# Recurrence scores by head parity: two 64-row products in two PSUM banks for one 128-row product over zeroed halves

## The chip, the cores and the metric

One core of one Trainium2 chip runs the whole program in one launch. The time is device microseconds from start to end. Three runs of the kernel before took 2598.1, 2588.69 and 2594.0 us, median 2594.0.

Engine names are those of the profile: PE is TensorE's matrix products, PEld its weight loads, DVE VectorE, ACT ScalarE, POOL GpSimd, SP SyncE. SP computes nothing here; it issues nearly all DMA transfers, in the order of its queue. The waits and counts of instructions are read from the profile and from the order in which the program lists each engine's instructions.

## The reference

One step of a two-layer decoder trunk: sliding-window attention, then RWKV-7 time mixing, over one prompt of 2048 tokens (16 learned meta tokens ahead of it) and a sample batch of 8 sequences of 4 tokens with a given state. The change lies in the time mixing. For every head (16 heads of 64) it runs a recurrence over the tokens:

```
def step(S, inp):
    r_t, w_t, k_t, v_t, a_t, b_t = inp
    sa = jnp.einsum('bhvk,bhk->bhv', S, a_t)
    S = S * w_t[:, :, None, :] + sa[..., None] * b_t[:, :, None, :] + v_t[..., None] * k_t[:, :, None, :]
    return S, jnp.einsum('bhvk,bhk->bhv', S, r_t)
```

Here w, k, v, r, a and b come from projections of the normalised input. After it come a group norm, a bonus term, a SiLU gate, the output projection, the residual add and the final norm.

## The kernel before

The program has three stages: the attention layer, the projections of the time mixing (their results go to DRAM), and from about 1600 us on the recurrence with everything behind it.

**Units and chunks.** The recurrence runs in chunks of 32 tokens, since inside a chunk it can be written as matrix products. There are 17 prompt units in order: unit 0 (kind `m`, 32 rows with the meta tokens) and units 1 to 16 (kind `p`, 128 tokens, four chunks each), and one sample unit (kind `s`). A unit goes through these steps:

1. `load_vectors` (L892 to L914) loads, for all heads, BK (the b and k vectors, 64 columns a chunk, two heads on 128 partitions: the head's parity e says which half) and L, one tile for a block of two chunks. L holds the a and r vectors of a head on the 64 partitions of its parity; the other 64 partitions are set to zero on POOL (L911, at raised priority, two memsets of 64x1024 for each block, four a unit).
2. `scores` (L930 to L955) multiplies BK with L for each pair of heads: K is 128 (both heads), and the zeroed halves keep the heads apart, so that the 128 columns of the result are the 64 scores of each head. Half of a block (four pairs) fills one PSUM bank `pz`. ACT copies one quadrant of it to LAs (32x128, eight copies a block), and DVE writes the masked scores to the half of L that was zero (64x256, eight operations a block). From here on L is one operand of 128 rows for the chain.
3. `inverse` (L957 to L1009): SP stores LAs to DRAM (`la_d<-LAs`, two transfers) and loads it back with one 32x32 matrix of a head and chunk on each partition (`LA<-la_d`, two). POOL multiplies by norms (`LA<-LA,ln`), makes the inverse of the unit triangular matrices in 31 steps of two operations each (`XT<-LA,X`, then `X<-X,XT`), and multiplies by norms again (`X<-X,ln`). SP stores the result (`tt_d<-X`, two transfers). Units 1 and 2 are done on DVE.
4. `elementwise` (L1302) drives steps 1 to 3 for a unit ahead and loads the inverse back as `TT<-tt_d`, two transfers of 64x512.
5. `keys` (L1342 to L1360) transposes BK on PE (L1357) into a bank `kt` of a PSUM pool `pk` of its own, and ACT copies it to LS.
6. `chain` (L1388) does a chunk: C = L times the state Z on PE, R0s by ACT, the solve `C<-R0s,TT` with the unit's inverse, the result into Z by ACT, then the new state `C<-Z,LS` on PE and its decay on DVE. `outputs` multiplies L with Z into Y.

**What sets the order.** The main loop (L1690 and below) goes through units and chunks. Beside unit i it puts in the group norm and gate of unit i - 1, the output projection of unit i - 2 (chunks 0 and 1; its end has three small `ms` operations on POOL, L1639, at raised priority) and, as `ahead`, the scores and inverse of unit i + 2. POOL therefore works on the inverse of one unit while PE runs the chain of an earlier one. The final order of each engine's instructions, SP's queue included, is decided by a scheduler when the program is built, from priorities, dependencies and free buffers; each engine then runs its list in order. An issue on SP that has to wait holds back everything behind it in SP's list. SP's issues also use eight semaphores in turn, so an issue waits until the one eight places ahead of it has landed.

**PSUM.** In the recurrence: `pz` one bank (scores), `pk` one (key copies), `pf` two (projections), `pr` four (C0, C1, Y0, Y1). Scores of the first units borrow banks of `pf` and `pr` (`bank`, L1259).

Of the kernel before, what the change touches and what calls it, by code (L numbers as in the profile page):

```python
# [30 lines left out]
def tile_hybrid_step(ctx: ExitStack, tc: tile.TileContext, a, o, c):  # L31
# [5 lines left out]
    def mm(out, lhsT, rhs, start, stop, **kw):  # L37
        return t_.matmul(out=out, lhsT=lhsT, rhs=rhs, start=start, stop=stop, **kw).ins  # L38
# [4 lines left out]
    def tt(e, out, in0, in1, op):  # L43
        return e.tensor_tensor(out=out, in0=in0, in1=in1, op=op).ins  # L44
# [844 lines left out]
    def load_vectors(u):  # L889

        u.BK, u.L = [], []
        if u.kind != "p":  # L892
            room = wl.tile([P, 2, 2 * KC * 64], F32, name="rooml", tag="L", bufs=nbuf["L"])
            u.spare = room[:, 1, 512:768].rearrange("p (g v) -> p g v", v=64)
            u.BKs = room[:, 1, 0:512].rearrange("p (h g c x) -> p h g c x", h=2, g=4, c=1)
        for half in range(2):
            hs = slice(half * 4, half * 4 + 4)
            BK = es.tile([P, 4, 4, 64], F32, name="BK", tag="BK", bufs=nbuf["BK"]) if u.kind == "p" else u.BKs[:, half]
            dma(BK, bk_d[u.blk][:, hs, u.c0:u.c0 + u.nch, :])
            u.BK.append(BK)  # L900
        for c2 in range(u.np):
            if u.kind == "p":
                L = wl.tile([P, 2, 2, KC, 64], F32, name="L", tag="L", bufs=nbuf["L"])
            else:
                L = room[:, 0].rearrange("p (e c g x) -> p e c g x", e=2, c=1, g=KC)
            u.L.append(L)
            w, c0 = min(2, u.nch - 2 * c2), u.c0 + 2 * c2
            for e, ps_ in HS:

                with tc.high_priority(offset=5000):  # L910
                    g_.memset(L[OS[e], e], 0.0)  # L911
                dma(L[ps_, e].rearrange("p c g x -> p (c g x)"), ar_d[u.blk][ps_, c0:c0 + w].rearrange("p c g x -> p (c g x)"))
            yield 0.8

# [15 lines left out]
    def scores(u, c2):  # L930

        nch = u.nch
        mk = smk_s if u.kind == "s" else smk
        w = min(2, nch - 2 * c2)
        L = u.L[c2]
        for half in range(2):
            hs = slice(half * 4, half * 4 + 4)
            BK = u.BK[half]
            ps = bank(u)
            for j in range(4):  # L940
                for cc in range(w):
                    u.scored = mm(ps[64 * cc:64 * cc + 64, j], BK[:, j, 2 * c2 + cc, :], L[:, :, cc, half * 4 + j, :], True, True)
            for cc in range(w):
                r0 = 64 * cc
                for e in range(2):
                    la = u.LAs[32 * (1 - e):32 * (1 - e) + 32, half, 2 * c2 + cc]
                    if u.kind == "s":
                        tt(v_, la, ps[r0:r0 + 32, :, e, 0:32], smk_a[r0:r0 + 32, None, :].broadcast_to([32, 4, 32]), ALU.mult)
                    else:
                        act(la, ps[r0:r0 + 32, :, e, 0:32])  # L950
            for cc in range(w):
                r0 = 64 * cc
                for e in range(2):
                    tt(v_, L[OS[e], e, cc, hs, :], ps[r0:r0 + 64, :, e, :],
                       mk[r0:r0 + 64, None, :].broadcast_to([64, 4, 64]), ALU.mult)  # L955

    def inverse(u, room=None, ln=None):  # L957

# [61 lines left out]
    with ExitStack() as ph:  # L1020
# [144 lines left out]
        for x, b in enumerate(order):  # L1165
# [39 lines left out]
            if follow is None:  # L1205

                if delay:
                    todo.append((b, prv))
                    rest_v = rest_values()
                    fill(rest_v, V0)  # L1210
                wrx.close()
                es = wrx.enter_context(tc.tile_pool(name="es", bufs=1, side="right", reuse_waits="tile"))
                wl = wrx.enter_context(tc.tile_pool(name="wl", bufs=1, side="right", reuse_waits="tile"))
                for u in us[:PRE]:
                    for _ in load_vectors(u):
                        pass
                if nblk > 2:
                    bank = lambda u: pd.tile([P, 4, 2, 64], F32, name="pz", tag="pd")
                    las = wk.tile([P, 2048], F32, name="las", tag="dx", bufs=1)
                    room1 = wk.tile([P, 2, 1024], F32, name="room1", tag="xn", bufs=1)  # L1220
                    for i, x0, room in ((1, 0, room1), (0, 1024, None)):
                        u = us[i]
                        u.LAs = las[:64, x0:x0 + 256 * u.nch].rearrange("p (h c g i) -> p h c g i", h=2, g=4, i=32)
                        for c2 in range(u.np):
                            scores(u, c2)
                        inverse(u, room, las[:, x0 + 1024 - 32:x0 + 1024] if i == 0 else las[:, 1536:1568])
# [19 lines left out]
    with ExitStack() as ph:  # L1246
# [1 line left out]
        zs = ph.enter_context(tc.tile_pool(name="zs", bufs=1, reuse_waits="tile"))  # L1248
        wk = ph.enter_context(tc.tile_pool(name="wk3", bufs=1, reuse_waits="tile"))
        cs = ph.enter_context(tc.tile_pool(name="c3", bufs=1, reuse_waits="tile"))  # L1250
        pz = ph.enter_context(tc.tile_pool(name="pz", bufs=1, space=PSUM, reuse_waits="tile"))
        pk = ph.enter_context(tc.tile_pool(name="pk", bufs=1, space=PSUM, reuse_waits="tile"))
        pf = ph.enter_context(tc.tile_pool(name="pf", bufs=2, space=PSUM, reuse_waits="tile"))
        pr = ph.enter_context(tc.tile_pool(name="pr", bufs=1, space=PSUM, reuse_waits="tile"))
        SQ = 1
        early = [0]

        def bank(u):
            if u.idx >= PRE:  # L1259
                return pz.tile([P, 4, 2, 64], F32, name="pz", tag="pz")  # L1260
            early[0] += 1
            place_, tag = ((pf, "pd"), (pr, "Y0"), (pr, "Y1"), (pz, "pz"))[early[0] % 4]
            return place_.tile([P, 4, 2, 64], F32, name="pz", tag=tag)


        w_g, w_o = [], []
# [78 lines left out]
        def keys(u, c2):  # L1345

            w = min(2, u.nch - 2 * c2)
            if u.kind == "s":
                u.LS[c2] = [u.room[:, 1]]
            else:  # L1350
                u.LS[c2] = [LSs[(LScount[0] + cc) % 4] for cc in range(w)]
                LScount[0] += 2
            for half in range(2):
                hs = slice(half * 4, half * 4 + 4)
                ps = pk.tile([P, 4, 2, 64], F32, name="kt", tag="kt", bufs=1)
                for j in range(4):
                    t_.transpose(out=ps[:w * 64, j].rearrange("p e d -> p (e d)"),  # L1357
                                 in_=u.BK[half][:, j, 2 * c2:2 * c2 + w, :].rearrange("p c x -> p (c x)"), identity=ident)
                for cc in range(w):
                    for e in range(2):  # L1360
                        act(u.LS[c2][cc][OS[e], e, hs, :], ps[cc * 64:cc * 64 + 64, :, e, :])
# [147 lines left out]
        def new_state(u, old_state, ums, outs, so, Z, LS):  # L1509
            tags = [0]  # L1510

            def bank():

                places = [(pz, "pz"), (pk, "kt")] + ([(pr, "C0"), (pr, "C1")] if over else [])
                tags[0] += 1
                place_, tag = places[tags[0] % len(places)]
                return place_.tile([P, 4, P], F32, name="ns", tag=tag, bufs=1)

            for gr in range(KC):
                ST = old_state(gr, bank())  # L1520
                um = ums[gr % 2]
                for e in range(2):
                    tt(v_, um[OS[e]], Z[OS[e], e, gr, None, :].broadcast_to([64, NB, 64]),
                       bmk[OS[e]].unsqueeze(2).broadcast_to([64, NB, 64]), ALU.mult)
                Sp = bank().rearrange("p a b -> p (a b)")
                for e, ps_ in HS:
                    mm(Sp[ps_], LS[OS[e], e, gr, :], um[OS[e]].rearrange("p b v -> p (b v)"), True, True)
                tt(v_, ST, ST, Sp.rearrange("p (b v) -> p b v", v=64), ALU.add)
                tt(v_, ST, ST, u.pe[:, gr, :].unsqueeze(2).broadcast_to([P, NB, 64]), ALU.mult)
                ps = bank()  # L1530
                for bp in range(4):
                    t_.transpose(out=ps[:, bp, :], in_=ST[:, 2 * bp:2 * bp + 2].rearrange("p b v -> p (b v)"), identity=ident)
                sl = outs[gr % 2]
                act(sl.rearrange("p b e k -> p (b e k)"), ps.rearrange("p a b -> p (a b)"))
                for b2 in range(2):
                    for e in range(2):
                        g_.dma_start(out=so[b2, :, gr, :, e], in_=sl[b2 * 64:b2 * 64 + 64, :, e])
                if gr % 2 == 1:
                    yield 0.8
# [326 lines left out]
```

## Time and profile before

| | before |
|---|---|
| three runs, us | 2598.1, 2588.69, 2594.0 (median 2594.0) |
| profiled execution, us | 2605.2 |
| its span, us | 2603.1 |
| mean granted TensorE clock | 0.962 |
| PE busy, share of the span | 2345.8 us, 90% |
| DVE | 1666.8 us, 64% |
| ACT | 1218.3 us, 47% |
| POOL | 1121.7 us, 43% |
| POOL from 1812 to 2337 us (ten units) | 386.25 of 525 us |

How to read it: the profile is of one execution, so its own time (2605.2) stands beside the span that its rows cover. "Busy" counts instructions that compute, not waits. A row of a list of waits says which engine and tile waited, for what, for how long in all, how often, and the longest. A chain of waits follows the work back from an end to what released each step; its shares are shares of the stretch that was asked for. A row of the time line has start, duration, engine, line, operation, tiles and count, and in brackets the idle time before it with what ended it. A line such as L44 or L50 is that of a helper (`tt`, `dma`), so tiles tell more than lines. Numbers behind a tile's name are left out in the profile.

### The profile page before, as it was taken

The page shows a single profiled execution, that of the slowest core. Times are in us where ns is not written, and L with a number is a line of the kernel's source. Part 1 is how long each engine was busy: PE and PEld are TensorE (multiplying, and loading weights), DVE is VectorE, ACT ScalarE, POOL GpSimd, SP SyncE. Part 2 cuts the span into 40 slices and gives each one's busy share as a digit, 9 for nine tenths or more (in the row PEclk, how much of TensorE's full clock was granted, in tenths as well). Part 3 has the DMA queues.
Part 4 walks back from the last instruction along what each step waited for, and adds up shares of the span by engine and source line. Part 5 has one row for each costly group of instructions (what it writes and reads, how often), then busy time and mean ns, then how long its engine had stood idle before and what let it go on. Part 6 is the DMA issues. An engine that isn't in the chain of part 4 may idle for free.

```text
span 2603.1 us, 59317 instructions
## 1 busy us (share of the span) xinstructions
PE 2345.8 (90%) x23876; PEld 1630.3 (63%) x23876; DVE 1666.8 (64%) x3264; ACT 1218.3 (47%) x2994; POOL 1121.7 (43%) x1640
## 2 busy tenths in 40 slices
PE   6999999899999897999999998769889998899897
PEld 5877777777844445676667776446555555555553
DVE  6587674667748887666565655755565556555664
ACT  6676455565523334454344434344445443544432
POOL 4242122232112344433333325256777777766603
PEclk9999998999999998999999998889999999999898
DMA  8433222332447564322222227575444554454323
GB/s 201 122 106 111 64 74 70 130 98 73 156 113 235 201 224 141 107 85 86 102 93 86 83 84 191 140 190 131 116 116 125 126 128 106 121 129 124 80 56 83
DMA packets 346230, 312.88 MB, mean 120 GB/s; under 512 B 205546, under 2 KB 282218, under 8 KB 344131
## 3 DMA queue, kind: packets, MB, share of 16 engines
q1 hardware_dynamic: 344339, 305.30, 40.8%
q0 software_dynamic: 1616, 3.79, 0.6%
q8 instruction: 188, 3.08, 0.5%
q14 instruction: 87, 0.71, 0.1%
HBM read 191.15 MB, written 119.84 MB: 119 GB/s over the span
## 4 chain that ended last, share of the span: by engine, by line
PE 31%; POOL 21%; DVE 20%; DMA 11%; ACT 8%; issue 7%; SPq 3%; POOLq 0%; ACTq 0%; DVEq 0%
PE pd L38 22%; POOL X L44 6%; POOL XT L44 6%; DVE xm L47 5%; SPq L50 3%; DMA LA<-la_d 2%; DVE xpr L44 2%; PE po L38 2%; ACT ssb L41 2%; POOL var L44 2%; POOL L L911 2%; PE C L38 1%; DMA wst<-in_rwkv_w_in 1%; DMA x<-in_x_prompt 1%; PE sc L38 1%
## 5 line engine op out<-in xcount | busy, mean ns | idle before, releaser
L38 PEld LDWEIGHTS <-yp 128*128 128x128 f16 x1488 | 140.4, 99 | 168.1 <-issue 12.3
L47 DVE SCALAR_TENSOR_TENSOR xm<-dx,mu,xn 128x256 f32<-128x256 f32 (+2 forms) x432 | 200.3, 523 | 48.3 <-POOL dx L44 47.1
L44 POOL TENSOR_TENSOR XT<-LA,X 128x126 f32<-128x126 f32 (+24 forms) x458 | 199.1, 435 | 33.7
L44 POOL TENSOR_TENSOR X<-X,XT 128x126 f32<-128x126 f32 (+24 forms) x458 | 199.0, 435 | 32.8
L38 PE MATMUL pd<-wg,xg 128*128 128x512 f16 (+1 forms) x816 | 199.8, 391 | 0.0
L38 PE MATMUL pd<-xp,wq 128*128 128x256 f16 (+2 forms) x1728 | 186.3, 266 | 13.9 <-DVE qp L47 8.9
L38 PE MATMUL pd<-xp,wg 128*128 128x256 f16 (+2 forms) x1728 | 188.7, 271 | 1.2 <-DVE xp L44 0.8
L38 PE MATMUL po<-wo,yp 128*128 128x512 f16 x768 | 187.5, 387 | 0.6 <-DVE yp L47 0.6
L38 PE MATMUL pd<-wvv,xpr 128*128 128x512 f16 (+1 forms) x816 | 186.9, 386 | 0.0
L38 PE MATMUL pd<-xpr,w 128*128 128x256 f16 (+2 forms) x1728 | 186.3, 267 | 0.0
L44 POOL TENSOR_TENSOR ssb<-ssb,bias 128x512 f32<-128x512 f32 x64 | 86.3, 1354 | 221.8 <-DVE ssb L462 178.3
L38 PEld LDWEIGHTS <-wq 128*128 128x128 f16 x1728 | 159.4, 99 | 35.6 <-DVE qp L47 10.4
L38 PE MATMUL pd<-xpr,wkk 128*128 128x256 f16 (+2 forms) x1728 | 179.5, 264 | 0.0
L38 PEld LDWEIGHTS <-wg 128*128 128x128 f16 x1728 | 162.2, 101 | 25.2 <-issue 4.5
L38 PEld LDWEIGHTS <-w 128*128 128x128 f16 x1728 | 157.7, 99 | 27.1 <-issue 9.7
L38 PEld LDWEIGHTS <-wkk 128*128 128x128 f16 x1728 | 158.2, 98 | 15.6 <-issue 0.4
L44 POOL TENSOR_TENSOR ps<-wst,ps 128x1024 f16<-128x1024 f32 x32 | 69.4, 2169 | 226.6 <-ACT wst L41 207.5
L38 PE MATMUL pd<-w,yp 128*128 128x512 f16 x720 | 162.3, 383 | 3.8 <-DMA yp<-y 3.8
L44 DVE TENSOR_TENSOR Z<-C,pe 64x256 f32<-64x256 f32 x256 | 107.8, 421 | 68.2 <-PE C L38 62.1
L38 PEld LDWEIGHTS <-xpr 128*128 128x128 f16 (+1 forms) x816 | 78.6, 100 | 101.8 <-issue 16.5
L44 DVE TENSOR_TENSOR L<-pz,smk 64x256 f32<-64x256 f32 x256 | 108.0, 422 | 47.8 <-ACT LAs L41 29.4
L44 DVE TENSOR_TENSOR xpr<-xm,xpr 128x512 f16<-128x512 f32 (+2 forms) x144 | 98.5, 705 | 57.3 <-ACT xpr L41 57.0
(358 smaller groups left out, 4983.4 us busy)
## 6 DMA issues: line engine op xcount, KB each, us to landing
wst<-in_rwkv_w_in SPq DMA_DIRECT2D x32, 512.0 KB
wsp<-ps SPq DMA_DIRECT2D x32, 512.0 KB
BK<-bk SPq DMA_DIRECT2D x32, 512.0 KB
L<-ar SPq DMA_DIRECT2D x64, 256.0 KB
x<-in_x_prompt SPq DMA_DIRECT2D x29, 512.0 KB
xn<-xn SPq DMA_DIRECT2D x14, 1028.0 KB
ar<-aro SPq DMA_DIRECT2D x28, 512.0 KB
bk<-bko SPq DMA_DIRECT2D x28, 512.0 KB
```

The costliest lines, as they stand in the source:

```text
L38: return t_.matmul(out=out, lhsT=lhsT, rhs=rhs, start=start, stop=stop, **kw).ins
L41: return s_.activation(out=out, in_=in_, func=func, **kw).ins
L44: return e.tensor_tensor(out=out, in0=in0, in1=in1, op=op).ins
L47: v_.scalar_tensor_tensor(out=out, in0=in0, scalar=scalar, in1=in1, op0=op0, op1=op1)
L50: return nc.sync.dma_start(out=out, in_=in_).ins
L911: g_.memset(L[OS[e], e], 0.0)
```

## The change

The zeroed halves are no longer written: L911 and its priority block go. `scores` multiplies only the 64 partitions of one head at a time (K is 64, 64 columns), twice as many products, the two parities in turn, each into its own bank, so that a block needs two banks at once where half a block needed one. ACT and DVE then work on whole blocks: four copies of 32x256 and four masked writes of 64x512 a block instead of eight of each. The PSUM pool `pz` gets two banks and takes over the key copies of `pk`, which goes. `bank` becomes `banks`; the sample's state update uses the two banks of `pz` where it used `pz` and `pk`.

```diff
             for e, ps_ in HS:
-                with tc.high_priority(offset=5000):
-                    g_.memset(L[OS[e], e], 0.0)
                 dma(L[ps_, e].rearrange("p c g x -> p (c g x)"), ar_d[u.blk][ps_, c0:c0 + w].rearrange("p c g x -> p (c g x)"))
...
-        for half in range(2):
-            hs = slice(half * 4, half * 4 + 4)
-            BK = u.BK[half]
-            ps = bank(u)
-            for j in range(4):
-                for cc in range(w):
-                    u.scored = mm(ps[64 * cc:64 * cc + 64, j], BK[:, j, 2 * c2 + cc, :], L[:, :, cc, half * 4 + j, :], True, True)
+        pss = banks(u)
+        for g in range(KC):
             for cc in range(w):
...
-                    la = u.LAs[32 * (1 - e):32 * (1 - e) + 32, half, 2 * c2 + cc]
...
-                        act(la, ps[r0:r0 + 32, :, e, 0:32])
...
+                for e, ps_ in HS:
+                    u.scored = mm(pss[e][64 * cc:64 * cc + 64, g, :], u.BK[g // 4][ps_, g % 4, 2 * c2 + cc, :], L[ps_, e, cc, g, :], True, True)
+        for cc in range(w):
+            r0 = 64 * cc
+            for e in range(2):
+                la = u.LAs[32 * (1 - e):32 * (1 - e) + 32, :, 2 * c2 + cc]
+                sc = pss[e][r0:r0 + 32, :, 0:32].rearrange("p (h g) i -> p h g i", h=2)
...
+                    act(la, sc)
+        for cc in range(w):
+            r0 = 64 * cc
+            for e in range(2):
+                tt(v_, L[OS[e], e, cc], pss[e][r0:r0 + 64], mk[r0:r0 + 64, None, :].broadcast_to([64, KC, 64]), ALU.mult)
...
-        pz = ph.enter_context(tc.tile_pool(name="pz", bufs=1, space=PSUM, reuse_waits="tile"))
-        pk = ph.enter_context(tc.tile_pool(name="pk", bufs=1, space=PSUM, reuse_waits="tile"))
+        pz = ph.enter_context(tc.tile_pool(name="pz", bufs=2, space=PSUM, reuse_waits="tile"))
...
-        def bank(u):
-            if u.idx >= PRE:
-                return pz.tile([P, 4, 2, 64], F32, name="pz", tag="pz")
+        def banks(u):
             early[0] += 1
-            place_, tag = ((pf, "pd"), (pr, "Y0"), (pr, "Y1"), (pz, "pz"))[early[0] % 4]
-            return place_.tile([P, 4, 2, 64], F32, name="pz", tag=tag)
+            places = ((pr, "Y0"), (pr, "Y1")) if u.idx < PRE and early[0] % 2 else ((pz, "pz"), (pz, "pz"))
+            return [place_.tile([P, KC, 64], F32, name="pz", tag=tag) for place_, tag in places]
...
-                ps = pk.tile([P, 4, 2, 64], F32, name="kt", tag="kt", bufs=1)
+                ps = pz.tile([P, 4, 2, 64], F32, name="kt", tag="pz")
```

Since a scheduler decides the order, the change also moves instructions that it doesn't name. SP's queue around the end of an inverse, in the middle of the recurrence, reads before (`out_y_prompt` stores a finished tile of the output, `h` is the residual that the next projection adds to, `Z` the v vectors of a chunk):

```order
L50 DMA out_y_prompt<-h_22067 128x1024
L50 DMA la_d<-LAs 32x32x32 x2
L50 DMA tt_d<-X 64x16x32 x2
L50 DMA h_22758<-h_4_87 128x1024
L50 DMA LA<-la_d 64x1024 x2
L50 DMA TT<-tt_d 64x1x512 x2
L50 DMA Z_19040<-v_106 32x512
```

The scores of the next unit go to DRAM ahead of the finished inverse. The same place now, in one of the four patterns that repeat from unit 4 on (the L that stands between is the load of a later unit; `pe` and `bont` are two small ones):

```order
L50 DMA tt_d<-X 64x16x32 x2
L50 DMA Z_19045<-v_106 32x512
L50 DMA Z_19046<-v_106 32x512 x2
L50 DMA L<-ar_157 64x1024
L50 DMA TT<-tt_d 64x1x512 x2
L50 DMA la_d<-LAs 32x32x32 x2
L50 DMA L<-ar_157 64x1024
L50 DMA out_y_prompt<-h_22138 128x1024
L50 DMA pe<-pe_170 128x32
L50 DMA bont<-bo_206 128x16
L50 DMA LA<-la_d 64x1024 x2
```

tt_d has moved ahead of la_d and TT ahead of LA, with other loads between. In the shortest of the four patterns the place reads:

```order
L50 DMA tt_d<-X 64x16x32 x2
L50 DMA L<-ar_158 64x1024
L50 DMA la_d<-LAs 32x32x32 x2
L50 DMA TT<-tt_d 64x1x512 x2
L50 DMA out_y_prompt<-h_23544 128x1024
L50 DMA L<-ar_158 64x1024
L50 DMA LA<-la_d 64x1024 x2
```

Of the other two, one has both TT ahead of la_d and fewer loads, one both TT ahead of la_d and more. In every one of them tt_d stands first.

POOL's list near the end of an inverse, before:

```order
L44 TENSOR_TENSOR XT<-LA,X 128x13x7
L911 MEMSET L 64x1024 x2
L44 TENSOR_TENSOR X<-X,XT 128x13x7
L1639 TENSOR_SCALAR ms_25068<-ssq_24832 128x2
L44 TENSOR_TENSOR XT<-LA,X 128x13x6
L44 TENSOR_TENSOR ms_25068<-ms_25068 128x1
L44 TENSOR_TENSOR X<-X,XT 128x13x6
L44 TENSOR_TENSOR ms_25068<-ms_25068,mhalf 128x1
L44 TENSOR_TENSOR XT<-LA,X 128x14x5
```

And now, from the last steps of an inverse to the first of the next:

```order
L44 TENSOR_TENSOR XT<-LA,X 128x16
L44 TENSOR_TENSOR X<-X,XT 128x16
L44 TENSOR_TENSOR X<-X,ln 128x512
L1634 TENSOR_SCALAR ms_25191<-ssq_24951 128x2
L44 TENSOR_TENSOR ms_25191<-ms_25191 128x1
L44 TENSOR_TENSOR ms_25191<-ms_25191,mhalf 128x1
L44 TENSOR_TENSOR LA<-LA,ln 128x1024
L44 TENSOR_TENSOR XT<-LA,X 128x31
```

The memsets are gone, and the three ms operations (L1634 is the old L1639) have moved from inside the inverse to the place between two inverses.

More of the change, by code (lines that the diff above doesn't have):

```diff
@@ L935, in scores @@
         L = u.L[c2]
-        for half in range(2):
-            hs = slice(half * 4, half * 4 + 4)
-            BK = u.BK[half]
-            ps = bank(u)
-            for j in range(4):
-                for cc in range(w):
-                    u.scored = mm(ps[64 * cc:64 * cc + 64, j], BK[:, j, 2 * c2 + cc, :], L[:, :, cc, half * 4 + j, :], True, True)
-            for cc in range(w):
-                r0 = 64 * cc
-                for e in range(2):
-                    la = u.LAs[32 * (1 - e):32 * (1 - e) + 32, half, 2 * c2 + cc]
-                    if u.kind == "s":
-                        tt(v_, la, ps[r0:r0 + 32, :, e, 0:32], smk_a[r0:r0 + 32, None, :].broadcast_to([32, 4, 32]), ALU.mult)
-                    else:
-                        act(la, ps[r0:r0 + 32, :, e, 0:32])
[L951 to L955, printed above, removed]
+        pss = banks(u)
+        for g in range(KC):
+            for cc in range(w):
+                for e, ps_ in HS:
[5 more added lines that the diff above has]
+                sc = pss[e][r0:r0 + 32, :, 0:32].rearrange("p (h g) i -> p h g i", h=2)
+                if u.kind == "s":
+                    for half in range(2):
+                        tt(v_, la[:, half], sc[:, half], smk_a[r0:r0 + 32, None, :].broadcast_to([32, 4, 32]), ALU.mult)
+                else:
+                    act(la, sc)
[3 more added lines that the diff above has]
+                tt(v_, L[OS[e], e, cc], pss[e][r0:r0 + 64], mk[r0:r0 + 64, None, :].broadcast_to([64, KC, 64]), ALU.mult)
     def inverse(u, room=None, ln=None):
@@ L1217, in tile_hybrid_step @@
                 if nblk > 2:
-                    bank = lambda u: pd.tile([P, 4, 2, 64], F32, name="pz", tag="pd")
+                    banks = lambda u: [pd.tile([P, KC, 64], F32, name="pz", tag="pd") for _ in range(2)]
                     las = wk.tile([P, 2048], F32, name="las", tag="dx", bufs=1)
@@ L1512, in bank @@
             def bank():
-                places = [(pz, "pz"), (pk, "kt")] + ([(pr, "C0"), (pr, "C1")] if over else [])
+                places = [(pz, "pz"), (pz, "pz")] + ([(pr, "C0"), (pr, "C1")] if over else [])
                 tags[0] += 1
                 place_, tag = places[tags[0] % len(places)]
-                return place_.tile([P, 4, P], F32, name="ns", tag=tag, bufs=1)
+                return place_.tile([P, 4, P], F32, name="ns", tag=tag)
             for gr in range(KC):
```

## The prediction

> **What bounds the kernel now.** The page's slices come first: they show that the last 40% of the program is a different program.
>
> ```profile
> PE   6999999899999897999999998769889998899897
> ...
> POOL 4242122232112344433333325256777777766603
> ```
>
> POOL is at four tenths or less in the first 24 slices and at six or seven in 11 of the last 14, the recurrence. PE looks full in both. A change to the recurrence is paid for there, so next comes the table of stretches, from the start of unit 5's inverse to the start of unit 15's, ten units. Its columns are the stretch, its length, busy us of PE, PEld, DVE, ACT and POOL, then granted clock, DMA share and GB/s.
>
> ```profile
> 1812.00:2337.00 525.00, 472.25 (x6957) 303.82 (x6957) 310.25 (x549) 242.76 (x660) 386.25 (x730) 0.97 0.50 122
> ```
>
> A unit takes 52.5 us; PE is busy for 47.2 of them, DVE 31.0, ACT 24.3, POOL 38.6. PE is the fullest but has 5 us to spare. Two lists of waits, POOL's from 1800 to 2370 and PE's from 2000 to 2400, and the chain from 2000 to 2072 say which engine sets the period:
>
> ```profile
> POOL LA L44 <- DMA LA<-la_d: 104.3, 11, 15.6
> ```
>
> ```profile
> PE pz L38 <- POOL X L44: 14.8, 7, 2.4
> PE pz L38 <- issue: 7.9, 5, 2.1
> PE kt L1357 <- ACT LS L41: 7.2, 13, 0.6
> PE C L38 <- DMA TT<-tt_d: 2.1, 1, 2.1
> ```
>
> ```profile
> by line: POOL X L44 29.1%; POOL XT L44 24.6%; DMA LA<-la_d 16.0%; issue 8.8%; POOL L L911 7.9%; SPq L50 7.6%; POOL var L44 4.0%; POOL LA L44 2.7%; POOL ms L44 1.9%; POOL ms L1639 0.6%; POOL var L1564 0.3%; POOLq L44 0.1%; POOLq L911 0.1%
> ```
>
> The chain holds no PE at all. It is POOL's inverse (X, XT), what else POOL does meanwhile (memsets of L911, ms, var), and the trip of the next unit's scores through DRAM (SPq, la_d, LA). So the period is one inverse plus one **gap**: POOL's idle time from its last operation on X to its first on the next LA. One of the eleven gaps is 15.6, the other ten share 88.7: 8.87 each. The rows of SP's queue and POOL around one of them (start, duration):
>
> ```profile
> 2008.68 1.35 SPq L50 DMA_DIRECT2D la_d<-LAs  x2
> 2012.42 1.35 SPq L50 DMA_DIRECT2D tt_d<-X  x2
> 2013.86 0.64 SPq L50 DMA_DIRECT2D h<-h  x1
> 2014.60 1.12 SPq L50 DMA_DIRECT2D LA<-la_d  x2
> 2015.81 1.09 SPq L50 DMA_DIRECT2D TT<-tt_d  x2
> ```
>
> ```profile
> 2021.82 1.92 POOL L44 TENSOR_TENSOR LA<-LA,ln 128x1024 f32<-128x1024 f32 x1 [9.43 <-DMA LA<-la_d]
> ```
>
> POOL ended at 2012.39. la_d had gone out 3.7 us earlier, under the inverse; only LA is in the gap, and it goes out ahead of TT. Remember this order.
>
> **What the change removes.** In POOL's groups from 1812.4 to 2350:
>
> ```profile
> L911 POOL MEMSET L<- 64x1024 f32 x42 | 39.7, 945 | 2.4
> L44 POOL TENSOR_TENSOR ms<-ms,mhalf 128x1 f32<-128x1 f32 x10 | 5.6, 561 | 0.0
> L44 POOL TENSOR_TENSOR ms<-ms 128x1 f32<-128x1 f32 x10 | 1.9, 194 | 0.0
> L1639 POOL TENSOR_SCALAR ms<-ssq 128x2 f32<-128x2 f32 x10 | 1.9, 192 | 0.9
> ```
>
> The memsets stand inside the inverses, four to a unit, on the path: all 42 go, **-39.7 us**. The three ms operations, 0.94 us a unit, stand inside the inverse too; in the new order POOL has them between its last X and the next LA, where it is idle anyway: 11 units, **-10.3**. While they ran, something stretched one X operation beside them. Its rows, and the one before it:
>
> ```profile
> 2059.78 0.32 POOL L44 TENSOR_TENSOR XT<-LA,X 128x70 f32<-128x70 f32 x1
> 2060.18 1.19 POOL L44 TENSOR_TENSOR X<-X,XT 128x70 f32<-128x70 f32 x1
> ```
>
> The same shape costs 0.87 more. The stretch follows the last ms, which releases a DVE operation; if it moves along, up to 9.6 go over 11 units, if it only moves elsewhere, none: I take half, **-4.8**. An inverse thus falls from 52.5 - 8.9 = 43.6 to about 38.6.
>
> **What PE, ACT and DVE get.** Scores were 32 products of 64x128 a unit and become 64 of 64x64. The first row is half a block of scores (8 products; the trace counts each twice), the second 16 products of the new shape, from the sample's state update near the end:
>
> ```profile
> 2044.11 1.09 PE L38 MATMUL pz<-L,BK 128*64 128x128 f32 x16 [2.06 <-issue]
> ...
> 2446.85 1.15 PE L38 MATMUL pz<-room,room 64*64 64x64 f32 x32
> ```
>
> Four rows of 1.09 become four of 1.15: +0.24 us a unit, on an engine with 5 us to spare. The waits ahead of pz and kt (14.8 + 7.9 + 7.2 us in 7.6 units, 3.9 each) should shrink, since a block's scores come in one group into two banks; PE then waits for TT instead. ACT copies and DVE masks the same elements in half as many instructions, with 28 and 21 us a unit idle as cover. All this is nothing while POOL's loop is longer than PE's 47.2; if POOL fell below that, it would be the bound.
>
> **What the change moves.** The scores of both blocks end earlier or later in PE's program, and SP's queue is re-ordered with them: in every unit from 4 on, tt_d (which waits for POOL's last X) now stands ahead of la_d, and TT ahead of LA. SP issues in order, so la_d, whose data is there, is locked behind the end of the inverse, and the whole trip falls into the gap. The trace has two such places, at units 5 and 16. SP's and POOL's rows at the first, and the last two transfers of the chain there:
>
> ```profile
> 1796.92 1.35 SPq L50 DMA_DIRECT2D tt_d<-X  x2
> 1798.69 1.00 SPq L50 DMA_DIRECT2D la_d<-LAs  x2
> 1799.80 0.70 SPq L50 DMA_DIRECT2D h<-h  x1
> 1801.04 1.13 SPq L50 DMA_DIRECT2D TT<-tt_d  x2
> 1802.35 1.13 SPq L50 DMA_DIRECT2D LA<-la_d  x2
> ```
>
> ```profile
> 1812.44 1.91 POOL L44 TENSOR_TENSOR LA<-LA,ln 128x1024 f32<-128x1024 f32 x1 [15.55 <-DMA LA<-la_d]
> 2397.57 1.91 POOL L44 TENSOR_TENSOR LA<-LA,ln 128x1024 f32<-128x1024 f32 x1 [16.34 <-DMA LA<-la_d]
> ```
>
> ```profile
> 1799.14 3.20 DMA la_d<-LAs
> ...
> 1802.90 9.32 DMA LA<-la_d
> ```
>
> Queued before TT, LA lands faster; and TT, when something waits for it, takes longest (from the chains at LA of unit 10 and at TT of unit 11):
>
> ```profile
> 2068.72 5.06 DMA LA<-la_d
> ```
>
> ```profile
> 2174.76 11.61 DMA TT<-tt_d
> ```
>
> So a gap of 15.55 and of 16.34 is measured for "tt_d, la_d, TT, LA". The new order has that in one unit of four (I take 16, two of the eleven gaps). In another, both TT stand ahead of la_d (17, three gaps), and in two of four there are four to six further issues ahead of LA as well. There la_d cannot go before TT, which needs tt_d landed: TT went out 4.15 us after POOL's end at unit 5. Add 1.13 for TT's issues, 3.65 from la_d's first issue to its landing (1798.69 to 1802.34), 0.55 to LA's second issue, and 5.06 to 9.32 for it: 14.5 to 18.8. An issue of SP also waits until the transfer eight places before it has landed, by the program's semaphores, and in these units that is TT for LA: 4.7 to TT's second issue, 8 (an estimate between 5.06 and 11.61) to its landing, 0.55 and 5.06 give 18.3, and with 11.61 it is 21.9. I take 18.5, six gaps. That is 2 x 16 + 3 x 17 + 6 x 18.5 = 194 for the gaps from unit 6 to 16, mean 17.6, where 10 x 8.87 + 16.34 = 105 stood: **+89** (+70 at 15.95 each, +115 at 20).
>
> The Trainium skill prices a transfer much lower: its page "DMA: Bandwidth & Descriptors", section "Anatomy of one DMA", fits 2.0 us plus bytes over 436 GB/s for transfers issued from GpSimd, which would make a gap in that order 7.8 us, an estimate, and the change a gain limited by PE, near 2536; the rows above for LA and TT disagree by two to five times.
>
> **Start and end.** Units 1 to 4 start the loop. The LA of unit 4 came almost for free and will now be locked in:
>
> ```profile
> 1698.90 1.91 POOL L44 TENSOR_TENSOR LA<-LA,ln 128x1024 f32<-128x1024 f32 x1 [9.63 <-DMA LA<-la_d]
> ...
> 1752.96 1.91 POOL L44 TENSOR_TENSOR LA<-LA,ln 128x1024 f32<-128x1024 f32 x1 [1.84 <-DMA LA<-la_d]
> ```
>
> That is +14 (16 for 1.84), less two inverses shortened by 4.7 each, less up to 9.6 in front of unit 3, whose scores PE now has earlier: **-4** (-9 to +9). At the end, PE comes to unit 16's solve 15.3 us after SP's issue of its TT, which takes some 12 (11.61):
>
> ```profile
> 2443.97 1.08 SPq L50 DMA_DIRECT2D TT<-tt_d  x2
> ```
>
> ```profile
> 2459.24 0.90 PE L38 MATMUL C<-R0s,TT 32*32 32x64 f32 x32
> ```
>
> so about 3 us of lateness there cost nothing, and the last inverse loses 0.94: **-4** (0 to -7).
>
> **The sum**: 89 - 39.7 - 10.3 - 4.8 - 4 - 4 = **+26 us**, at 52.5 + 8.7 - 5 = 56 us a unit. The profiled execution took 2605.2 us (span 2603.1), 11 over the median of 2594.0, and becomes 2631; the median becomes **2620**. The removed work is worth 63 us; the change breaks even at a mean gap of (105 + 63) / 11 = 15.3 us.
>
> **The rivals.** *The gap is only what was seen*: all eleven stay at the 15.95 of the two places, the further issues being hidden under la_d's own trip. +70 - 63 = +7: 2601, no change by the 0.3% (7.8 us) that a measurement of this kernel can tell. For it: it is measured. Against: in three orders of four, more stands ahead of LA than at those places. *Faster*: the 9.3 us of LA came from colliding with TT, and where TT has landed before LA goes out, or goes out long before it, LA takes the 5.06 of its usual place: 1.35 + 1.0 + 3.2 + 0.55 + 5.06 = 11.2, say 11.5, and 11 x 11.5 - 105 - 63 = -41: 2553. It decides at a gap below 15.3. Against: where both TT stand first, waiting for tt_d's landing replaces the collision. *The cleanest form of it*, gaps left at 8.9 and PE's 47.2 the bound, is excluded as long as SP keeps the order that the program now has; -58, 2536. *Slower still*: in the two long orders LA waits for a TT that takes its full 11.61: 22 there, 18.5 and 16 in the others, 219.5 in all: +51, 2645.
>
> **How the numbers follow.** Forecast 0.58, gap as seen 0.20, faster 0.12, clean 0.02, slower still 0.08. The range is from 2582, the seen gap with the stretched operation and start at their best ends, to 2646, the long orders at their worst; it leaves out the two fast cases and a little above. Its likeliest part is 2604 to 2636. Faster by over 0.3%: 0.12 + 0.02 + 0.02 from the lower end of the others, 0.16. Within 0.3%: 0.20. Slower: 0.64.
>
> **What would show it.** Right: L911 gone from POOL; tt_d ahead of la_d on SP in every unit; POOL idle for 15.5 to 20 us ahead of each LA, the two long orders longest; 38 to 39 us from LA to the last X; PE's waits for pz gone and a wait of about 8 us a unit for TT in their place. Wrong: gaps under 15.3, an inverse that stays above 42, or PE still without waits for TT, which would mean that PE had become the bound.

## The result, and the profile after

The changed kernel takes 2658.59 us (median of 4 runs, 2652.97 to 2659.8) where the kernel before takes 2595.76 (median of 4): 2.4% slower, ratio 1.0240, 95% interval 1.0222 to 1.0257. The forecast was slower by 26 us, in a range up to 2646; it is slower by 63. The direction was right, and so was the place, POOL's idle time ahead of LA; the size was less than half of what was measured.

The profiled execution took 2658.5 us (span 2656.7). Its span is 53.6 us longer than that of the profiled execution of before, 9 less than the medians differ by: the profiled execution of before, 2605.2, was a long one.

The stretch from the start of unit 5's inverse to that of unit 15's, ten units again (columns as before the change):

```profile
1819.00:2390.00 571.00, 482.48 (x7594) 302.16 (x7594) 304.87 (x470) 229.42 (x578) 332.50 (x690) 0.89 0.45 113
```

It lasts 571 us instead of 525: a unit takes 57.15 us (2390.67 - 1819.13 by ten), not 52.5. POOL is busy 33 us a unit instead of 39, and the granted clock of PE is 0.89 instead of 0.97. POOL's waits from 1800 to 2420:

```profile
POOL LA L44 <- DMA LA<-la_d: 184.5, 11, 18.3
POOL ms L1634 <- ACT sq L41: 18.8, 9, 2.2
```

LA is waited for 184.5 us instead of 104.3, and on top of that POOL's ms operations, which now stand in the gap, wait for ACT. POOL's rows at one gap and at the two ends of the eleven:

```profile
1819.13 1.91 POOL L44 TENSOR_TENSOR LA<-LA,ln 128x1024 f32<-128x1024 f32 x1 [15.38 <-DMA LA<-la_d]
...
2083.81 1.26 POOL L44 TENSOR_TENSOR X<-X,ln 128x512 f32<-128x512 f32 x1
2105.44 1.91 POOL L44 TENSOR_TENSOR LA<-LA,ln 128x1024 f32<-128x1024 f32 x1 [17.09 <-DMA LA<-la_d]
...
2449.92 1.91 POOL L44 TENSOR_TENSOR LA<-LA,ln 128x1024 f32<-128x1024 f32 x1 [17.77 <-DMA bont<-bo]
```

From the end of the last X (2085.07) to LA are 20.4 us. The bracket counts 17.1 of them, since the ms operations lie between. Taken this way, the eleven gaps ahead of units 6 to 16 sum to 221 us (105 before, as the forecast counted them), and the inverses of units 5 to 15 to 410 (480 before): 20.1 and 37.3 us each. SP's queue in that gap:

```profile
2085.10 1.35 SPq L50 DMA_DIRECT2D tt_d<-X  x2
2086.54 2.02 SPq L50 DMA_DIRECT2D Z<-v  x4
2088.66 1.12 SPq L50 DMA_DIRECT2D TT<-tt_d  x2
2089.83 3.14 SPq L50 DMA_DIRECT2D la_d<-LAs  x2
2093.01 3.82 SPq L50 DMA_DIRECT2D L<-ar  x1
2096.93 0.53 SPq L50 DMA_DIRECT2D out_y_prompt<-h  x1
2097.50 1.72 SPq L50 DMA_DIRECT2D L<-ar  x1
2099.34 1.17 SPq L50 DMA_DIRECT2D LA<-la_d  x2
```

tt_d is ahead of la_d and TT ahead of LA, as the order showed. But two things were not in the forecast's picture. The issues behind TT are slow: la_d takes SP 3.1 us (1.35 in the gap shown of before), 2.7 of them its second issue, and the two loads of L 3.8 and 1.7 us, where two loads of L earlier in the unit, at 2052.83 and 2054.51, took 0.45 and 0.51. So LA leaves 14.3 us after POOL's end, 9.5 after la_d. SP's list of waits for this gap (2084.9 to 2106) holds, beside tt_d's 3.1 us for the inverse, one row:

```profile
SPq L50 <- DVE Z L44: 0.4, 1, 0.4
```

The time in the gap is that of the issues themselves; why they take so long, no run here shows. The second thing is that ACT wrote the scores late:

```profile
2086.43 0.63 ACT L41 ACTIVATE sq<-h 128x512 f32<-128x512 f32 x1 [17.61 <-DVE ytm L44]
...
2087.18 1.55 ACT L41 ACTIVATE LAs<-pz 32x256 f32<-32x256 f32 x4
```

The copies to LAs end at 2088.73, 3.7 us after the inverse. The prediction had said of la_d "whose data is there". In this order it is not: the copies stand on ACT behind sq, which waits for the end of the group norm's additions (ytm) on DVE, because sq uses the one buffer (tag `ysq`) that the group norm's squares and v vectors use. In this order, though, it costs little: SP was busy with TT until 2089.78 and la_d left at 2089.83, and in all eleven gaps la_d left within 0.5 us of the end of the issue ahead of it.

The forecast had PE waiting about 8 us a unit for TT. It waits about 5 for R0s instead, which stands on ACT behind those copies (PE's waits from 1800 to 2420, then its rows):

```profile
PE C L38 <- ACT R0s L41: 55.7, 22, 5.8
```

```profile
2062.86 1.16 PE L38 MATMUL pz<-L,BK 64*64 64x64 f32 x64
...
2067.55 2.12 PE L38 MATMUL po<-wo,yp 128*128 128x512 f16 x9
...
2089.18 1.50 PE L38 MATMUL C<-R0s,TT 32*32 32x64 f32 x32 [4.43 <-ACT R0s L41]
2090.62 4.02 PE L38 MATMUL pd<-wg,xg 128*128 128x512 f16 x9
```

The chain of waits from 2080 to 2106 joins the two: from ACT's copies and R0s over PE's products and DVE's Z to an issue on SP, the second load of L, and from there to LA. Its last piece ahead of SP (start, duration):

```profile
2096.91 0.44 DVE Z L44
```

That link is thin. DVE's Z ended at 2097.35, but SP was issuing out_y until 2097.46 in any case, and its wait for Z is the 0.4 us of the list above. What keeps LA back here are the issues in front of it.

### The profile page after: what moved, and what is told of

The parts are those of the page before. It is cut to its first block, busy times and chain, and to the rows that moved or that the text cites. A ratio compares the mean times of both kernels' runs of the same rounds, so it can differ in the third digit from the quotient of the medians.

```text
span 2656.7 us, 61111 instructions
## 1 busy us (share of the span) xinstructions
PE 2343.7 (88%) x24932; PEld 1622.3 (61%) x24932; DVE 1652.0 (62%) x3132; ACT 1197.9 (45%) x2864; POOL 1044.9 (39%) x1572
## 4 chain that ended last, share of the span: by engine, by line
PE 30%; DVE 21%; POOL 16%; DMA 12%; ACT 9%; issue 8%; SPq 4%; POOLq 0%; ACTq 0%; DVEq 0%
PE pd L38 21%; POOL X L44 5%; DVE xm L47 4%; POOL XT L44 4%; SPq L50 4%; DMA LA<-la_d 3%; PE po L38 2%; DVE xpr L44 2%; PE C L38 2%; DMA la_d<-LAs 2%; ACT ssb L41 2%; DMA wst<-in_rwkv_w_in 1%; PE sc L38 1%; POOL var L44 1%; DVE ytm L44 1%
## 5 line engine op out<-in xcount | busy, mean ns | idle before, releaser
L38 PE MATMUL pd<-wg,xg 128*128 128x512 f16 (+1 forms) x816 | 227.6, 431 | 0.0
L44 POOL TENSOR_TENSOR XT<-LA,X 128x126 f32<-128x126 f32 (+24 forms) x458 | 184.1, 402 | 46.5 <-DMA wo<-wsp 11.5
L38 PE MATMUL po<-wo,yp 128*128 128x512 f16 x768 | 180.9, 380 | 0.6 <-DVE yp L47 0.6
L38 PE MATMUL C<-R0s,TT 32*32 32x64 f32 x2080 | 74.4, 237 | 91.5 <-ACT R0s L41 63.0
L41 ACT ACTIVATE sq<-h 128x512 f32<-128x512 f32 (+1 forms) x34 | 21.4, 629 | 280.9 <-DVE ytm L44 225.7
L38 PEld LDWEIGHTS <-xg 128*128 128x128 f16 (+1 forms) x816 | 80.6, 107 | 104.5 <-issue 42.5
```

Source lines behind the costliest of these rows:

```text
L41: return s_.activation(out=out, in_=in_, func=func, **kw).ins
```

## The experiments

Ten kernels ran, each beside the kernel before, whose median was 2594 to 2598 us each time.

**e1: la_d first.** Two theories were to be told apart: SP's order alone makes the loss, or the scores are late and would hold la_d in any order. The changed kernel, with the tt_d and TT of a unit emitted in the next unit's `inverse`:

```diff
+        prev = held.pop() if held else None
+        if prev is not None:
+            with tc.issue_after(lad):
+                store_tt(prev)
...
+        if prev is not None:
+            with tc.issue_after(lal):
+                load_tt(prev)
```

`prev` is the unit ahead, `lad` and `lal` are the last la_d and LA of this unit; `store_tt` and `load_tt` issue tt_d and TT as before.

> The changed kernel, with the store of a unit's inverse (tt_d) issued on SP only after the next unit's la_d, and TT only after its LA, for units 3 to 15; nothing else is edited. Queue theory (SP's order alone locks the trip of the scores into the gap): la_d goes out under the inverse again, the gap falls from 20 us to 9 to 12, a unit takes 47 to 50 us instead of 57, and the time is 2555 to 2590, below the kernel before. Rival (the scores themselves are late, because ACT copies them to LAs only after the group norm has ended, so that la_d could not go much sooner in any order): la_d still goes out within 2 us of the end of the inverse; only LA's landing gets shorter without TT ahead of it, a unit takes 50 to 54 us, and the time is 2590 to 2630.

Measured: 2596.77 us, ratio to before 1.0017 (1.0001 to 1.0033), 62 us under the changed kernel. Nothing of the loss is left, to 0.3%. SP, ACT and POOL in one gap:

```profile
2059.18 0.94 SPq L50 DMA_DIRECT2D la_d<-LAs  x2
...
2060.88 1.55 SPq L50 DMA_DIRECT2D tt_d<-X  x2
2062.53 1.49 SPq L50 DMA_DIRECT2D LA<-la_d  x2
```

```profile
2057.61 1.54 ACT L41 ACTIVATE LAs<-pz 32x256 f32<-32x256 f32 x4
```

```profile
2054.25 1.26 POOL L44 TENSOR_TENSOR X<-X,ln 128x512 f32<-128x512 f32 x1
...
2067.90 1.91 POOL L44 TENSOR_TENSOR LA<-LA,ln 128x1024 f32<-128x1024 f32 x1 [9.11 <-DMA LA<-la_d]
```

Neither theory is right alone. The order was worth the 62 us, and more in the gap: ahead of units 6 to 16 it is 12.4 to 13.5 us where the changed kernel has 20.1 on average, while the inverse became 3 us longer (39.7 to 40.5), 1.8 to 2.4 of them a wait of POOL for DVE's sum of the variance. But la_d still leaves 3.7 us after the inverse's end (2055.51), the moment its scores are there (2059.15): the gap here is 12.4, not 9, and the time is in the rival's range.

**e2: la_d behind, in the kernel before.** The reverse: nothing of the change but its order.

```diff
+        with tc.issue_after(last_tt[0]) if last_tt and u.idx > 4 else ExitStack():
             for e in range(2):
                 dma(la_d[e].rearrange("l j i -> j l i"),
```

> The kernel before, with each unit's la_d (units 5 on) forced behind the tt_d of the unit ahead; memsets and scores as before. Queue theory: the gap goes from 8.9 to about 16 in eleven places, so +70 to +85 us: 2665 to 2680, as slow as or slower than the changed kernel, since the memsets are still there. Rival (the order only shows that scores are late, and costs little where they are early): la_d loses only the 3.7 us that it had in hand, +30 to +45: 2625 to 2640.

Measured: 2665.1 us, ratio 1.0276 (1.0257 to 1.0294), +71 us, the queue theory's number. SP, ACT and POOL:

```profile
2082.02 1.35 SPq L50 DMA_DIRECT2D tt_d<-X  x2
2083.46 1.29 SPq L50 DMA_DIRECT2D la_d<-LAs  x2
```

```profile
2078.45 1.10 ACT L41 ACTIVATE LAs<-pz 32x128 f32<-32x128 f32 x4 [4.63 <-PE pz L38]
```

```profile
2097.64 1.91 POOL L44 TENSOR_TENSOR LA<-LA,ln 128x1024 f32<-128x1024 f32 x1 [15.65 <-DMA LA<-la_d]
```

Here the scores are there at 2079.55, before tt_d goes, and still the gap is 15.65; the eleven ahead of units 6 to 16 are 14.8 to 17.4, 16.6 on average. The gap of this order by itself is thus what the two places in the trace of before had shown, 15.55 and 16.34. The changed kernel's 20.1 has 3.5 us more.

**e3 and e4: the group norm's power left out.** ACT's copies are late because of the group norm, and that waits for two POOL operations (the power -1/2 of the variance) queued in the inverse. So they were left out, in the changed kernel (e3) and in e1 (e4):

```diff
-            with tc.high_priority(offset=5000):
-                g_.tensor_scalar(out=var[:n], in0=var[:n], scalar1=1.0 / 64, scalar2=64e-5, op0=ALU.mult, op1=ALU.add)
-                tt(g_, var[:n], var[:n], mhalf[:n], ALU.pow)
+            v_.tensor_scalar(out=var[:n], in0=var[:n], scalar1=1.0 / 64, scalar2=64e-5, op0=ALU.mult, op1=ALU.add)
```

> The changed kernel with the two POOL operations of the group norm (the power -1/2 of the variance) left out and one DVE operation in their place, so the group norm is computed without that power; SP's order has la_d behind tt_d and TT as in the changed kernel. Queue theory: POOL's inverse loses 3 us a unit and the gap stays near 20: -30 to -35 us, 2624 to 2630. Rival (late scores): scores come 5 to 8 us earlier, and the gap gets shorter as well, to 15 or 16: -70 to -85 us, 2575 to 2590.

> Both edits: la_d ahead of tt_d and LA ahead of TT, and no power of the variance on POOL (that power is left out of the group norm). Queue theory: compared with la_d first alone it gains 3 us a unit at most, until PE's 46 to 47 us a unit are the bound: 2545 to 2565. Rival: this is where the large step comes, 30 to 60 us below la_d first alone, to the same 2545 to 2565.

e3 measured 2659.31 us (1.0245, 1.0222 to 1.0269): no gain at all, a miss for both theories. Scores were early (2059.73), the inverse 3 us shorter (34.5), and the gap grew to 22 to 25. Its SP queue, ACT and POOL:

```profile
2070.36 1.35 SPq L50 DMA_DIRECT2D tt_d<-X  x2
2073.71 1.10 SPq L50 DMA_DIRECT2D TT<-tt_d  x2
...
2078.90 3.84 SPq L50 DMA_DIRECT2D la_d<-LAs  x2
```

The chain of waits there (2069 to 2096) holds the trip of TT:

```profile
2074.29 8.12 DMA TT<-tt_d
```

```profile
2058.19 1.54 ACT L41 ACTIVATE LAs<-pz 32x256 f32<-32x256 f32 x4
```

```profile
2095.04 1.91 POOL L44 TENSOR_TENSOR LA<-LA,ln 128x1024 f32<-128x1024 f32 x1 [23.52 <-DMA BK<-bk]
```

la_d has had its data for 19 us and leaves 8.6 us after the inverse, behind TT, which waits for tt_d, and behind out_y. By the chain the second la_d then waits for TT to land, 8.1 us. So late scores are not needed for the loss: with early ones the queue takes more. e4 measured 2561.44 us (0.9875, 0.9852 to 0.9897), 35 below e1. That is inside both theories' range, so it doesn't tell them apart.

**e5: a buffer of its own for sq.** e1 with one line changed, to free ACT's copies without leaving work out:

```diff
-            sq = wk.tile([P, 512], F32, name="sq", tag="ysq", bufs=SQ)
+            sq = wk.tile([P, 512], F32, name="sq", tag="sq", bufs=1)
```

> The changed kernel with la_d ahead of tt_d and LA ahead of TT (as e1), and the buffer of sq (the square of the residual, which ACT makes ahead of the copies to LAs) separated from the one that the group norm's ysq and vt use. If what is left of the gap in e1 (12.4 to 13.3 us, against 8.9 before) comes from ACT, where the copies to LAs stand behind an sq that waits for the group norm's last use of the shared buffer: LAs end 3 to 4 us sooner, the gap falls to 9 to 10, a unit takes 49 to 50 us and the time is 2555 to 2575. Rival: the copies are not what ends last, but the store of y (out_y), which waits for POOL's ms operations that now stand behind the inverse and holds back la_d on SP, as it does in e4: no change from e1, 2590 to 2600.

Measured: 2587.43 us (0.9968, 0.9948 to 0.9988): 9 below e1 and between the two ranges, so neither number came true. The mechanism is the rival's. The copies now end 2.7 us before the inverse (2044.07 and 2046.81), and la_d still leaves after it:

```profile
2048.95 0.36 SPq L50 DMA_DIRECT2D out_y_prompt<-h  x1
...
2049.89 1.49 SPq L50 DMA_DIRECT2D la_d<-LAs  x2
```

```profile
2047.05 0.56 POOL L44 TENSOR_TENSOR ms<-ms,mhalf 128x1 f32<-128x1 f32 x1
2060.19 1.91 POOL L44 TENSOR_TENSOR LA<-LA,ln 128x1024 f32<-128x1024 f32 x1 [12.59 <-DMA LA<-la_d]
```

out_y stores the tile that DVE scales with the result of ms, and ms now runs after the last X. Since out_y is ahead of la_d on SP, the three small operations that the forecast had called free in the gap hold back the scores.

**e9: out_y behind LA.** e5 with the store of y handed over to the next `inverse`:

```diff
+                elif u.idx + 5 < len(us):
+                    outs.append((o["y_prompt"][0, (t - 1) * P:t * P, :], h1))
...
                 load_tt(prev)
+                while outs:
+                    dma(*outs.pop())
```

> e5 with one more move on SP: the store of a finished tile of y (out_y) is issued behind the LA of the unit ahead instead of ahead of its la_d, for all but the last tiles. Theory (in e5 la_d stands behind out_y, which waits for POOL's ms operations at the end of the inverse, 3 us after the scores and the inverse are ready): la_d goes out before the inverse ends, the gap falls from 13.4 us to 9 or 10, a unit takes 47.5 to 49 us, PE near its bound, and the time is 2540 to 2565, below both kernels. Rival (LA's landing or PE's own waits hold the unit at 51 us whatever SP does): 2575 to 2590, as e5.

Measured: 2553.43 us, ratio 0.9834 (0.9819 to 0.9848): about 43 us faster than the kernel before, 105 than the changed one. SP in one gap, and the stretch from 1819 to 2319, ten units and a bit:

```profile
2079.16 1.20 SPq L50 DMA_DIRECT2D la_d<-LAs  x2
2080.45 1.54 SPq L50 DMA_DIRECT2D tt_d<-X  x2
2083.14 1.13 SPq L50 DMA_DIRECT2D LA<-la_d  x2
2084.36 0.54 SPq L50 DMA_DIRECT2D out_y_prompt<-h  x1
```

```profile
1819.00:2319.00 500.00, 458.00 (x7860) 293.17 (x7855) 309.94 (x484) 234.84 (x591) 353.64 (x711) 0.99 0.53 130
```

The inverse takes 37.4 us on average, the gap of units 6 to 15 10.4 to 12.0, a unit 47.7 to 50.2, and PE is busy 92% at a clock of 0.99. The time is in the range, the mechanism came only in part: la_d goes 2.6 us after the inverse's end (2076.56), not before it, because its scores end at 2077.44 and loads of L and two small ones stand ahead of it; LA leaves 5.6 to 6.9 us after the end where e5 has 7.3 to 9.2. So the removal of the memsets can pay once SP's queue lets it through. How much of the 43 us the memsets give isn't shown: the kernel before was not run with out_y behind LA and a buffer of its own for sq.

**e6, e7, e8: the parts of the change.** e6 puts the memsets back into the changed kernel; e7 has the 64-row products without memsets in the old PSUM pools, one parity after the other in the one bank of pz; e8 has only the PSUM pools of the change.

e6, against the changed kernel:

```diff
+                with tc.high_priority(offset=5000):
+                    g_.memset(L[OS[e], e], 0.0)
```

e7, against the kernel before:

```diff
-                with tc.high_priority(offset=5000):
-                    g_.memset(L[OS[e], e], 0.0)
...
+        for e, ps_ in HS:
+            ps = bank(u).rearrange("p g e x -> p (g e) x")
+            for g in range(KC):
+                for cc in range(w):
+                    u.scored = mm(ps[64 * cc:64 * cc + 64, g, :], u.BK[g // 4][ps_, g % 4, 2 * c2 + cc, :], L[ps_, e, cc, g, :], True, True)
```

e8, against the kernel before:

```diff
-        pz = ph.enter_context(tc.tile_pool(name="pz", bufs=1, space=PSUM, reuse_waits="tile"))
-        pk = ph.enter_context(tc.tile_pool(name="pk", bufs=1, space=PSUM, reuse_waits="tile"))
+        pz = ph.enter_context(tc.tile_pool(name="pz", bufs=2, space=PSUM, reuse_waits="tile"))
...
-                ps = pk.tile([P, 4, 2, 64], F32, name="kt", tag="kt", bufs=1)
+                ps = pz.tile([P, 4, 2, 64], F32, name="kt", tag="pz")
```

> The changed kernel with the 64 memsets of the zero halves put back (the products do not need them). The plan's order differs too: with them the first la_d stands ahead of tt_d again, the second behind it. Theory (the change lost by SP's order, and the memsets were worth their 3.8 us a unit): the inverse takes 41 us instead of 37.2, the gap is 14 to 16 instead of 20, a unit takes 56 to 58 and the time is 2640 to 2665, about that of the changed kernel although POOL has 60 us more to do. Rival (order is of no account, the memsets are on the path): 2695 to 2705.

> The kernel before with the products of 64 rows and no memsets, but without the rest: one parity at a time in the one bank of pz, copies and masks behind it, key copies in their own pool. Its order has tt_d ahead of la_d, and one la_d or both behind TT. Theory: the removal of the memsets alone turns SP's order round, and that is the loss: 2640 to 2670, as the changed kernel. Rival (the loss comes from the two banks and the shared pool, which bring the scores of a block in one late group): near or below the kernel before, 2550 to 2600.

> The kernel before with only the PSUM part of the change: pz has two banks, shared by scores (half a block each), key copies and the sample's state; products, zeroed halves and memsets as before. Its order keeps la_d ahead of tt_d in every second unit and splits the pair in the others. Theory: as fast as before where the order is kept, 3 to 6 us a unit slower in the split units: 2595 to 2625. Rival (the pool is the loss): 2640 or more.

e6: 2646.95 us (1.0191, 1.0158 to 1.0224); inverse 41.5 to 42.6 and gap 14.7 to 16.7 from unit 7 on. With 60 us more for POOL to do it is no slower than the changed kernel, because the gap is shorter. Its own units say why. Ahead of unit 6 stands the changed kernel's order, TT before la_d and a load of L between la_d and LA; ahead of unit 7 la_d comes before TT, and no load of L follows:

```profile
1851.99 3.44 SPq L50 DMA_DIRECT2D la_d<-LAs  x2
1855.48 3.18 SPq L50 DMA_DIRECT2D L<-ar  x1
...
1861.68 1.11 SPq L50 DMA_DIRECT2D LA<-la_d  x2
...
1909.22 1.30 SPq L50 DMA_DIRECT2D la_d<-LAs  x2
...
1912.97 1.19 SPq L50 DMA_DIRECT2D LA<-la_d  x2
```

From la_d to LA are 9.7 us and 3.75 us, and the gaps are 19.3 and 15.5. In units 9 to 15 the first la_d stands ahead of tt_d too, and the gap hardly changes (14.7 to 15.8).

e7: 2660.86 us (1.0242, 1.0211 to 1.0274), the changed kernel's time without its two banks and shared pool. e8: 2605.15 us (1.0028, 1.001 to 1.0046), and an experiment within one run, because its order has la_d ahead of tt_d in every second unit:

```profile
1844.27 2.30 POOL L44 TENSOR_TENSOR LA<-LA,ln 128x1024 f32<-128x1024 f32 x1 [8.43 <-issue]
1902.65 1.91 POOL L44 TENSOR_TENSOR LA<-LA,ln 128x1024 f32<-128x1024 f32 x1 [16.01 <-DMA LA<-la_d]
```

From the end of the last X the gap is 7.9 to 10.5 us where la_d is first and 15.2 to 17.2 where tt_d is. All kernels here that keep the memsets have at least one la_d ahead of tt_d in some or all units, unless forced; all that drop them have tt_d first, unless forced. So tt_d in first place in every unit goes with the removal of the memsets, and the banks alone (e8) cost 7 to 11 us. But e6 has the memsets and is still about 50 us above the kernel before. So the rest of the change, the 64-row products with their copies of whole blocks, alone or together with the banks, has a part in the order too. It was not run alone with the memsets, and why the scheduler turns the order was not tried.

**e10: parity by parity.** The products of a block in another order, to settle their price on PE:

```diff
-        for g in range(KC):
-            for cc in range(w):
-                for e, ps_ in HS:
+        for e, ps_ in HS:
+            for g in range(KC):
+                for cc in range(w):
```

> The changed kernel with the 32 products of a block issued parity by parity instead of in turn. If the 1.16 us for a block's 32 products come from pairs on the two halves of the rows running side by side, a block takes 2.2 to 2.3 us here, 2.2 us a unit more on PE; the time stays 2650 to 2665, since PE is not what the unit waits for. Rival (the products of 64 columns are just cheaper than the row of the sample's state update showed): still 1.16 us.

```profile
2054.87 1.91 PE L38 MATMUL pz<-L,BK 64*64 64x64 f32 x64
```

2649.75 us (1.021, 1.0191 to 1.023): 9 below the changed kernel, at the edge of what can be told. A block takes 1.91 us parity by parity, less than expected but 0.75 more than in turn.

## Why the prediction came out short

Right: POOL's loop is the bound, the memsets and ms leave the inverse, SP's new order locks the scores' trip into the gap, and that costs more than the memsets gave. e1 (-62), e2 (+71) and the alternating gaps of e8 show the order's price directly. Of the 27.6 us that the profiled execution is above the forecast's sum (53.6 for 26):

- **The gap** was forecast at 194 us for eleven and is 221: +27. The step that failed is the term "3.65 from la_d's first issue to its landing", after which LA was to go. From la_d's first issue to LA's first are 8.3 to 11.0 us in nine of the eleven gaps, because la_d and the loads behind it are slow to issue. la_d lands late as well (9.2 us in unit 8, by the chain), but SP's waits for its landing sum to only 2.9 us from 1800 to 2430. The terms beside it held: TT went out 3.5 to 4.0 us after the end for 4.15, and in these nine gaps LA took 4.8 to 7.8 us from its first issue to POOL, inside or just below the forecast's 5.6 to 9.9 (0.55 and 5.06 to 9.32).

  Two experiments put a price on it. Against the order alone (e2, 16.6) the gap is 3.5 us longer, and unit 6 of e6 has 3.7 more than unit 7: that is the price of TT ahead of la_d and of the further issues. By pattern, the gaps are: the shortest 17.7 and 17.9 for 16; both TT ahead of la_d and the fewest further issues 20.4 to 20.9 for 17; out_y ahead of la_d as well 21.1 to 22.0 for 18.5; the fourth 19.2 to 20.0 for 18.5.

  "la_d, whose data is there" was wrong too, since the scores end 0.9 to 3.7 us after the inverse, but behind tt_d and TT that delayed la_d by less than 0.5 us; it counts only once the order is mended (e1).
- **The inverse** was forecast 5.0 us shorter and is 6.4 shorter: -15.5 over eleven. Stretched X and XT operations, of which the forecast counted one and took half, are nine of 62 in each inverse before (5.5 to 5.8 us over the shortest time of the same shapes) and six after in ten of the eleven (3.7 to 3.9): 20 us less in all, where 4.8 was forecast. The one at 70 elements is still there, in XT:

```profile
2078.97 1.19 POOL L44 TENSOR_TENSOR XT<-LA,X 128x70 f32<-128x70 f32 x1
```

  What stretches them was not tried.
- **The start** was forecast at -4 and is +6.7 (unit 5's LA at 1819.13, for 1812.44). Unit 3 began 12.9 us sooner, but its inverse then stood:

```profile
1699.45 0.59 POOL L44 TENSOR_TENSOR XT<-LA,X 128x31 f32<-128x31 f32 x1 [11.53 <-DMA wo<-wsp]
...
1764.92 1.91 POOL L44 TENSOR_TENSOR LA<-LA,ln 128x1024 f32<-128x1024 f32 x1 [21.90 <-DMA LA<-la_d]
```

  so 8.1 us of the lead were left at its end, and the gap ahead of unit 4 is 21.9 where 16 was assumed and 1.8 stood before.
- **The end** was forecast at -4 and is +1.3 (206.8 us from unit 16's LA, 205.5 before).

The rest of the miss, 11 us, is no term of the sum. The sum was added to a profiled execution of before that lay 11 us above its median, and the forecast took these off again, while the changed kernel's profiled execution lies at its median.

Two smaller steps failed without moving the sum. "All this is nothing" held for PE, but its price was wrong: a block of scores costs 1.16 us, 2.3 a unit, where 4.6 was forecast from a row of products that were not issued in pairs; in e7, where a parity's 16 products stand alone, they take 1.15 us, 2.3 a block. The Trainium skill, page "TensorEngine Tiling (Array Packing)", section "Theoretical Speedup", gives up to two times for a dimension of 64 or less; 1.16 against the 2.18 of the 128-row products is 1.9 times, so the trace agrees. With the parities in sequence (e10) it is 1.14 times. And "where it is idle anyway" for ms was true of POOL and false of SP's queue behind it (e5, e9).

The range failed at its upper end because its worst case was built from one thing, the landing of TT, and not from several that add: slow issues behind la_d in every pattern, and a start that doesn't pay. The inverse's extra 15.5 us were luck that hid part of this.

## What to carry to other kernels

When an edit shortens a loop whose next input travels through a queue that issues in order, read what the new program puts between the end of one turn and the issue of the next input: 6 us saved in each turn were lost, and 4 to 5 more, to issues that changed places. For each issue there, ask when its data is ready, what it waits for and how long it takes to go out, and add these, rather than assume that it hides. A small operation moved into an engine's idle time is free only if nothing in the queue ahead of the critical transfer waits for its result.

## What the runs showed of the hardware

A PE that has waited is slow afterwards. Behind the 4.4 us wait at 2089.18, nine products of 512 columns took 4.02 us where nine take 2.12 in the middle of work; the granted clock was 0.50 from 2089.18 to 2094.6 and 1.00 from 2067.5 to 2069.7. The ten waits for R0s of 4.35 us and more between 1819 and 2390 (4.35 to 5.8) were all followed by nine such products in 3.3 to 4.0 us. Over ten units the granted clock was 0.89 in the changed kernel, 0.97 before and 0.99 in e9. The Trainium skill's page "TensorE: Matmul & The Clock Gate", Part 1, has half the clock after an idle window of about 3.4 us. The ten waits agree with that, but a shorter one halved the clock too: behind the 2.59 us wait at 2020.45 it was 0.51 until 2027, where it had been 1.00 from 2012 to 2017. So in this kernel 2.6 us were enough. Each of the ten waits cost 1 to 2 us more in the nine products behind it. In the gap shown little of this reached LA, since SP waited only 0.4 us for what followed on DVE.
